# Loads of x behind later weight pieces, and half of its scaling on POOL, in a one-core hybrid retention and attention layer

## The chip, the core and the metric

The kernel runs on one core of a Trainium2 chip. The core has TensorE (PE, with its weight loads shown apart as PEld), VectorE (DVE), ScalarE (ACT), GpSimd (POOL) and SyncE (SP, which here only issues DMAs). Each engine takes its instructions in the order of its own queue and waits on semaphores for the others. The metric is device time in microseconds (us), smaller is better: the median of several runs.

## The reference

One decoder layer on x of 256 rows by 1024, in float32, with two branches that read the same normalised input:

```
h    = rmsnorm(x, ln_w)
proj = h @ w_in                    # 1024 x 9216: rq rk rv rg | mq mk mv mg | gr gm
ret  = groupnorm(retention(rq, rk, rv)) * silu(rg);  ret = ret @ w_ret_o
mo   = causal_attention(mq, mk, mv, ALiBi) * silu(mg);  mo = mo @ w_moba_o
y    = sigmoid(gr) * ret + sigmoid(gm) * mo
out  = rmsnorm(x + y @ w_out, final_norm_w)
```

Retention has 4 heads (queries and keys of 128, values of 256, chunks of 128 rows) with a fixed decay table. The attention has 8 heads of 128, and 256 rows are one block, so only the causal part of the own block is left.

## The kernel before

**Weights in groups and pieces.** All weights are cut into 24 groups of 512 columns, listed in `groups`. Groups 0 and 1 are the retention values, 2 its queries, 3 its keys, 4 the first half of the attention's queries, and so on. A group is loaded in four pieces of two 128-row blocks each (512 KB). Piece 2.1 below is piece 1 of group 2. The raw piece goes into one of 6 buffers, and `split` turns it into a rounded part wh (ACT, L108) and the remainder wl (DVE, L109). A raw buffer is free for the next load when L109 has read it. Products are three or two matmuls per block, so that the two parts together keep float32 accuracy.

**x before its norm is known.** Groups 0 to 2 are multiplied with x times `ln_w` alone (tiles x0, split in `split_x`), since the row factors rs come later. The rows of x (tile xn, two halves of 128 rows) are loaded by SP behind the second piece of group 1, at L133. `x_stats` squares and sums each half on ACT (L185), and a few tiny instructions make rs (L170 to L175). The values of groups 0 and 1 are scaled with rs when they leave PSUM (vh on ACT at L443, vl on DVE at L445). `x_stats_t` spreads rs over the partitions with two small matmuls and a copy to rsb on DVE (L195).

**x after the norm.** `norm_x(k)` makes the normalised block k of eight: z on DVE (L163, x times `ln_w` times rsb), the rounded part on ACT (L164), the remainder on DVE (L165). They are written to the tile xs, which every group from 3 to 17 reads. The queries of group 2, made from x0, are multiplied with rsb on DVE (L414) and split by L258 on ACT and L259 on DVE.

**PSUM and the order.** A group with flag T makes four outputs of 128 columns (f0 to f3), each in its own buffer of the PSUM pool ps_m, which has four. ACT reads one half of it (L393) and DVE adds the other (L395); then the buffer is free. So f0 of group 3 needs the buffer that f0 of group 2 had. The order of each engine's queue comes from a scheduler that takes the program and reorders it within its dependencies.

Of the kernel before, what the change touches and what calls it, by code (L numbers as in the profile page):

```python
# [23 lines left out]
F32 = mybir.dt.float32  # L24
F32R = mybir.dt.float32r
AF = mybir.ActivationFunctionType
ALU = mybir.AluOpType
# [6 lines left out]
NT = S // P  # L34
# [14 lines left out]
def hybrid_kernel(ctx: ExitStack, tc, xT, x, w_in, gn_w, w_ret_o, w_moba_o, w_out, fn_w, decay, out):  # L49
    nc = tc.nc  # L50
# [26 lines left out]
    def load(g, c):  # L77
        src = groups[g][0].rearrange("(k p) c -> p k c", p=P)
        t = wp.tile([P, 2, GW], F32, name="raw", tag="raw", bufs=6)
        raw[g, c] = t  # L80
        if g == 0:
            for j in range(2):
                k = 2 * c + j
                sx = slice(KT + k * S if k else 0, KT + (k + 1) * S)
                nc.sync.dma_start(xt[:, sx], xT[:, sx])
                for cs in cut(g, k):
                    nc.sync.dma_start(t[:, j, cs], src[:, k, cs])  # L87
        else:
            nc.sync.dma_start(t, src[:, 2 * c:2 * c + 2])
# [33 lines left out]
    lnw = xt[:, :KT]  # L123
# [3 lines left out]
    xn = ac.tile([P, NT, D], F32, name="xn", tag="xn")  # L127
    xr = x.rearrange("(t p) d -> p t d", p=P)
    for c in range(4):
        load(1, c)  # L130
        if c == 1:
            for t in range(NT):
                nc.sync.dma_start(xn[:, t], xr[:, t])  # L133
    dec = ac.tile([P, RET_HEADS * 3 * P], F32, name="dec", tag="dec")

    ident = cst.tile([P, P], F32, name="ident")
# [23 lines left out]
    def norm_x(k):  # L160
        xk, h, l = xt[:, KT + k * S:KT + (k + 1) * S], xs[:, k, 0], xs[:, k, 1]
        z = wk.tile([P, S], F32, name="z", tag="z", bufs=4)
        ins = nc.vector.scalar_tensor_tensor(z, xk, lnw[:, k:k + 1], rsb, op0=ALU.mult, op1=ALU.mult)  # L163
        nc.scalar.activation(h, z, AF.Copy)  # L164
        nc.vector.tensor_sub(l, z, h.bitcast(F32))  # L165
        return ins.ins

    def rsqrt(y, a, tmp):
# [9 lines left out]
    rsb = cst.tile([P, S], F32, name="rsb")  # L178
# [68 lines left out]
    def new_v(n, dt=F32):  # L247
        return ac.tile([P, GW], dt, name=n, tag="v", bufs=8)
# [8 lines left out]
    def split_to(out, a, eng=nc.gpsimd):  # L257
        nc.scalar.activation(out[:, 0], a, AF.Copy)  # L258
        eng.tensor_sub(out[:, 1], a, out[:, 0].bitcast(F32))  # L259
# [128 lines left out]
    def evac_t(g, i, ps):  # L388

        f = (i + 4) if g in (7, 8, 13, 15, 17, 19, 21) else i  # L390

        def halves(out, w=1.0):
            nc.scalar.activation(out, ps[:, 1], AF.Copy, scale=w)  # L393
            if w == 1.0:
                nc.vector.tensor_add(out, ps[:, 0], out)  # L395
            else:
                nc.vector.scalar_tensor_tensor(out, ps[:, 0], w, out, op0=ALU.mult, op1=ALU.add)

        def tmp(n):
            return wk.tile([P, S], F32, name=n, tag=n, bufs=4)  # L400

        if g in (4, 7):
            q = qT[g // 7][:, i]
            halves(q, 1.0 / math.sqrt(P))
            split_to(qs[g // 7][:, i], q[:, P:])
        elif g in (5, 8):
            k = kT[g // 8][:, i]
            halves(k)
            split_to(ks[g // 8][:, i], k)
        elif g in (2, 3):  # L410
            a = (qT if g == 2 else kT)["r"][:, i]
            halves(a)
            if g == 2:
                nc.vector.tensor_mul(a, a, rsb)  # L414
            split_to((qs if g == 2 else ks)["r"][:, i], a if g == 2 else a[:, :P], nc.vector)
        elif g in (12, 13):
            z, sg = tmp("z"), wk.tile([P, S], F32, name="sg", tag="sg", bufs=2)
            halves(z)
            nc.scalar.activation(sg, z, AF.Sigmoid)
            nc.vector.tensor_mul(z, z, sg)  # L420
            nc.vector.tensor_mul(oT[:, f], oT[:, f], z)
        elif g in (14, 15, 16, 17):
            z = tmp("z")
            halves(z)
            if i % 2 == 0:
                gt = new_v("gt")
                G[g // 16, f], G[g // 16, f + 1] = gt[:, :S], gt[:, S:]
            nc.scalar.activation(G[g // 16, f], z, AF.Sigmoid)
        elif g in (18, 19):
            halves(A[:, f])  # L430
            nc.gpsimd.tensor_mul(A[:, f], A[:, f], G[0, f])  # L431
        elif g in (20, 21):
            z = tmp("z")
            halves(z)
            nc.vector.tensor_mul(z, z, G[1, f])
            nc.vector.tensor_add(z, z, A[:, f])
            nc.scalar.activation(yT[:, f, 0], z, AF.Copy)
            nc.vector.tensor_sub(yT[:, f, 1], z, yT[:, f, 0].bitcast(F32))
# [31 lines left out]
    def unit(g, i):  # L470
# [25 lines left out]
        if groups[g][1] == "N":  # L496
            evac_n(g, i, proj_n(g, lambda k: xs[:, k], i))
        else:
            if g == 2:
                a = x0s  # L500
            elif g < 18:
                a = lambda k: xs[:, k]
            elif g < 20:
                a = lambda k: rT[k // 2][:, k % 2]
            else:
                a = lambda k: mT[k // 4][:, k % 4]
            for f in (2 * i, 2 * i + 1):
                evac_t(g, f, proj_t(g, a, f))
# [44 lines left out]
    for g in range(2):  # L553
        for i in range(2):
            stream(g, i)
        if g == 0:
            x_stats()
            nc.sync.dma_start(dec, decay)
        pair = [pm.tile([P, GW], F32, name="ps_m", tag="m") for t in range(NT)] if g else ps0
        last = proj_first(g, pair)  # L560
        for t in range(NT):
            evac_n(g, t, pair[t])
        if g:
            with tc.issue_after(last.ins):
                x_stats_t()
            begun = [norm_x(k) for k in range(KT)][3]
    for g in range(2, NG - 2):
        for i in range(2):
            u = 2 * g + i
            stream(g, i)  # L570
            if u == 38:

                xr = new_v("xr", F32R)
# [22 lines left out]
    for t in range(NT):  # L596
        part, a, s, y, v = (sc[:, t, j:j + 1] for j in range(5))
# [80 lines left out]
```

## Time and profile before

| | |
|---|---|
| median of 3 runs | 304.42 us (303.76 to 304.47) |
| profiled execution, its own time | 305.6 us |
| span of the profiled execution, first to last instruction | 302.7 us |
| mean granted TensorE clock | 0.994 |
| PE busy | 294.2 us (97%) |
| DVE busy | 220.7 us (73%) |
| ACT busy | 191.5 us (63%) |
| POOL busy | 28.6 us (9%) |

The profile is one execution. Its time is 2.9 us more than its span and 1.2 us above the median, so a difference that is worked out from it is added to the median. Times in a timeline count from the span's start. A timeline row gives the start, the time from the first start to the last end of the merged instructions, the engine, the line, the output and input names, and how many were merged; in brackets stands how long the engine sat idle before, and what ended the wait. Rows of one engine can overlap a little, because an instruction starts before the one ahead of it has fully ended: what one costs in a queue is the distance from start to start.

### The profile page before, as it was taken

Reading aid. Unit: us, or ns where it says so; the run is one execution under the profiler, and the core shown is the slowest. Engines: PE = TensorE matmul, PEld = TensorE weight load, DVE = VectorE, ACT = ScalarE, POOL = GpSimd, SP = SyncE. Lnnn points to the kernel's source line nnn. Section 1 sums busy time; section 2 is a strip of 40 time slices with the busy share of each in tenths; the row PEclk is TensorE's granted clock in tenths of the full one; section 3 lists DMA queues with packets and bytes.
Section 4 is the critical chain, followed back from the end, with each engine's and each line's share of the span. In section 5 each row is a group of like instructions: output and inputs, shape, how many; then the busy total and the mean of one; then the engine's idle time right before and its main releaser. Section 6 shows DMA issues by size and latency. Waiting matters only on the chain.

```text
span 302.7 us, 4547 instructions
## 1 busy us (share of the span) xinstructions
PE 294.2 (97%) x1628; PEld 253.1 (84%) x1628; DVE 220.7 (73%) x402; ACT 191.5 (63%) x365; POOL 28.6 (9%) x36
## 2 busy tenths in 40 slices
PE   8999989999999999999999999999999999999992
PEld 4768878999888899888888888888888888888891
DVE  3849999977699695884747899557657458899342
ACT  5778695665738676675965857757847626646231
POOL 3000000231200123200000000000000245000000
PEclk9999999999999999999999999999999999999997
DMA  6999847948174461735267185484475576440011
GB/s 184 340 397 410 309 136 222 316 154 240 51 260 126 162 209 71 246 113 197 56 221 237 44 261 146 149 279 120 157 228 174 158 252 229 143 142 1 0 69 69
DMA packets 28966, 55.08 MB, mean 182 GB/s; under 512 B 1936, under 2 KB 3984, under 8 KB 28944
## 3 DMA queue, kind: packets, MB, share of 16 engines
q1 hardware_dynamic: 28624, 54.54, 55.4%
q8 instruction: 12, 0.20, 0.3%
q10 hardware_dynamic: 288, 0.26, 0.2%
q14 instruction: 10, 0.08, 0.1%
q0 software_dynamic: 32, 0.00, 0.0%
HBM read 53.75 MB, written 1.05 MB: 181 GB/s over the span
## 4 chain that ended last, share of the span: by engine, by line
PE 89%; DMA 4%; ACT 3%; SPq 1%; DVE 1%; issue 1%; DVEq 0%; ACTq 0%
PE ps_m L233 37%; PE ps_m L234 19%; PE ps_m L218 7%; PE ps_m L220 7%; PE ps_m L219 7%; DMA raw<-in_w_in 2%; ACT wh L108 2%; DMA xt<-in_xT 2%; PE ps_m L206 1%; PE ps_m L207 1%; PE ps_m L205 1%; PE ps_t L285 1%; SPq L87 1%; ACT xs L164 1%; PE ps_s L264 1%
## 5 line engine op out<-in xcount | busy, mean ns | idle before, releaser
L233 PE MATMUL ps_m<-xs,wh 128*128 128x512 f32 x352 | 123.6, 393 | 0.8 <-ACT qT L393 0.8
L109 DVE TENSOR_TENSOR wl<-raw,wh 128x1024 fp32r<-128x1024 f32 x88 | 108.8, 1256 | 12.9 <-ACT wh L108 12.6
L234 PE MATMUL ps_m<-xs,wl 128*128 128x256 f32 x352 | 98.9, 282 | 0.0
L108 ACT ACTIVATE wh<-raw 128x1024 fp32r<-128x1024 f32 x88 | 90.5, 1053 | 7.2 <-DMA raw<-in_w_in 2.6
L233 PEld LDWEIGHTS ps_m<-xs,wh 128*128 128x128 f32 x352 | 66.0, 188 | 14.5 <-ACT qT L393 1.1
L234 PEld LDWEIGHTS ps_m<-xs,wl 128*128 128x128 f32 x352 | 66.5, 189 | 0.2
L218 PE MATMUL ps_m<-wh,xs 128*128 128x512 f32 x64 | 25.5, 398 | 0.0
L219 PE MATMUL ps_m<-wl,xs 128*128 128x512 f32 x64 | 25.3, 395 | 0.0
L220 PE MATMUL ps_m<-wh,xs 128*128 128x512 f32 x64 | 25.3, 395 | 0.0
L233 PE MATMUL ps_m<-rT,wh 128*128 128x512 f32 x64 | 22.2, 390 | 0.0
L233 PE MATMUL ps_m<-mT,wh 128*128 128x512 f32 x64 | 22.2, 390 | 0.0
L395 DVE TENSOR_TENSOR z<-ps_m,z 128x256 f32<-128x256 f32 x32 | 13.4, 419 | 11.8 <-ACT z L393 11.7
L393 ACT ACTIVATE z<-ps_m 128x256 f32<-128x256 f32 x32 | 12.1, 379 | 13.1 <-PE ps_m L234 12.9
L431 POOL TENSOR_TENSOR A<-A,gt 128x256 f32<-128x256 f32 x8 | 6.8, 855 | 120.1 <-DVE A L395 120.1
L234 PE MATMUL ps_m<-rT,wl 128*128 128x256 f32 x64 | 18.0, 282 | 0.0
L234 PE MATMUL ps_m<-mT,wl 128*128 128x256 f32 x64 | 18.0, 282 | 0.0
L220 PEld LDWEIGHTS ps_m<-wh,xs 128*128 128x128 f32 x64 | 12.0, 188 | 2.9
L206 PE MATMUL ps_m<-wl,x 128*128 128x512 f32 (+1 forms) x34 | 13.7, 404 | 0.5 <-DVE wl L109 0.5
L219 PEld LDWEIGHTS ps_m<-wl,xs 128*128 128x128 f32 x64 | 12.0, 188 | 2.5
L218 PEld LDWEIGHTS ps_m<-wh,xs 128*128 128x128 f32 x64 | 12.0, 188 | 2.5
L233 PEld LDWEIGHTS ps_m<-mT,wh 128*128 128x128 f32 x64 | 12.0, 188 | 2.5
L233 PEld LDWEIGHTS ps_m<-rT,wh 128*128 128x128 f32 x64 | 12.0, 188 | 2.5
(183 smaller groups left out, 487.2 us busy)
## 6 DMA issues: line engine op xcount, KB each, us to landing
raw<-in_w_in SPq DMA_DIRECT2D x68, 512.0 KB, 4.7
raw<-in_w_ret_o SPq DMA_DIRECT2D x8, 512.0 KB, 5.2
raw<-in_w_moba_o SPq DMA_DIRECT2D x8, 512.0 KB, 5.7
raw<-in_w_out SPq DMA_DIRECT2D x8, 512.0 KB, 5.2
raw<-in_w_in SPq DMA_DIRECT2D x7, 256.0 KB, 4.6
xn<-in_x SPq DMA_DIRECT2D x2, 512.0 KB, 8.6
xt<-in_xT SPq DMA_DIRECT2D x7, 128.0 KB, 4.7
dec<-in_decay SPq DMA_DIRECT2D x1, 768.0 KB, 9.3
```

The source lines that it names most:

```text
L87: nc.sync.dma_start(t[:, j, cs], src[:, k, cs])
L108: nc.scalar.activation(h, r, AF.Copy)
L109: nc.vector.tensor_sub(l, r, h.bitcast(F32))
L206: nc.tensor.matmul(ps[:, cs], xh, l, start=False, stop=False)
L218: nc.tensor.matmul(ps, a(k)[:, 0, sl], h, start=not begun and k == 0, stop=False)
L219: nc.tensor.matmul(ps, a(k)[:, 0, sl], l, start=False, stop=False)
L220: nc.tensor.matmul(ps, a(k)[:, 1, sl], h, start=False, stop=k == KT - 1)
L233: nc.tensor.matmul(ps, h, a(k), start=k == 0, stop=False)
L234: nc.tensor.matmul(ps[:, 0], l, a(k)[:, 0], start=False, stop=k == KT - 1)
L393: nc.scalar.activation(out, ps[:, 1], AF.Copy, scale=w)
L395: nc.vector.tensor_add(out, ps[:, 0], out)
L431: nc.gpsimd.tensor_mul(A[:, f], A[:, f], G[0, f])
```

## The change

SP loads the first half of the rows of x behind the third piece of group 1, and the second half behind the fourth. `norm_x` keeps its form for blocks 0 to 3. For blocks 4 to 7, z is x times rsb on POOL, and `ln_w` goes in as a scale of the ACT instruction and as the scalar of a three-operand DVE instruction, which replaces the plain subtraction. The product of group 2's queries with rsb goes from DVE to POOL.

```diff
     for c in range(4):
         load(1, c)
-        if c == 1:
-            for t in range(NT):
-                nc.sync.dma_start(xn[:, t], xr[:, t])
+        if c >= 2:
+            nc.sync.dma_start(xn[:, c - 2], xr[:, c - 2])
...
         z = wk.tile([P, S], F32, name="z", tag="z", bufs=4)
-        ins = nc.vector.scalar_tensor_tensor(z, xk, lnw[:, k:k + 1], rsb, op0=ALU.mult, op1=ALU.mult)
-        nc.scalar.activation(h, z, AF.Copy)
-        nc.vector.tensor_sub(l, z, h.bitcast(F32))
+        if k < 4:
+            ins = nc.vector.scalar_tensor_tensor(z, xk, lnw[:, k:k + 1], rsb, op0=ALU.mult, op1=ALU.mult)
+            nc.scalar.activation(h, z, AF.Copy)
+            nc.vector.tensor_sub(l, z, h.bitcast(F32))
+        else:
+            ins = nc.gpsimd.tensor_mul(z, xk, rsb)
+            nc.scalar.activation(h, z, AF.Copy, scale=lnw[:, k:k + 1])
+            nc.vector.scalar_tensor_tensor(l, z, lnw[:, k:k + 1], h.bitcast(F32), op0=ALU.mult, op1=ALU.subtract)
         return ins.ins
...
             if g == 2:
-                nc.vector.tensor_mul(a, a, rsb)
+                nc.gpsimd.tensor_mul(a, a, rsb)
             split_to((qs if g == 2 else ks)["r"][:, i], a if g == 2 else a[:, :P], nc.vector)
```

The scheduler orders the queues anew. Lines behind the first edit are one lower in the changed kernel, and from the second half of `norm_x` on four higher. ACT's queue from the pieces of group 1 to the first values, before (wh is a weight piece, junk the squares of one half of x, vh the values):

```order
L108 ACTIVATE wh<-raw 128x1024 x2
L185 ACTIVATE junk,ss<-xn 128x1024 x2
L170 ACTIVATE sst<-ss 128x2
L108 ACTIVATE wh<-raw 128x1024
L443 ACTIVATE vh<-ps_m,rs 128x512
```

And now:

```order
L108 ACTIVATE wh<-raw 128x1024 x3
L189 ACTIVATE junk,ss<-xn 128x1024
L108 ACTIVATE wh<-raw 128x1024
L189 ACTIVATE junk,ss<-xn 128x1024
L174 ACTIVATE sst<-ss 128x2
L108 ACTIVATE wh<-raw 128x1024
L447 ACTIVATE vh<-ps_m,rs 128x512
```

Two weight pieces have gone ahead of the second square. DVE's queue from the last pieces of group 2 to the first queries of group 2 that leave PSUM and what follows them, before (vl is the remainder of the values, xs that of the normalised x, wl that of a weight piece, rqs that of the queries):

```order
L445 SCALAR_TENSOR_TENSOR vl<-ps_m,rs,vh 128x512
L109 TENSOR_TENSOR wl<-raw,wh 128x1024
L445 SCALAR_TENSOR_TENSOR vl<-ps_m,rs,vh 128x512
L195 COPY rsb<-ps_s 128x256
L163 SCALAR_TENSOR_TENSOR z<-xt,rsb 128x256 x4
L109 TENSOR_TENSOR wl<-raw,wh 128x1024
L165 TENSOR_TENSOR xs<-z,xs 128x256 x4
L163 SCALAR_TENSOR_TENSOR z<-xt,rsb 128x256 x3
L165 TENSOR_TENSOR xs<-z,xs 128x256 x2
L163 SCALAR_TENSOR_TENSOR z<-xt,rsb 128x256
L109 TENSOR_TENSOR wl<-raw,wh 128x1024
L165 TENSOR_TENSOR xs<-z,xs 128x256 x2
```

And now, with the rows up to the next pieces of group 3:

```order
L449 SCALAR_TENSOR_TENSOR vl<-ps_m,rs,vh 128x512 x2
L199 COPY rsb<-ps_s 128x256
L163 SCALAR_TENSOR_TENSOR z<-xt,rsb 128x256 x3
L165 TENSOR_TENSOR xs<-z,xs 128x256 x3
L163 SCALAR_TENSOR_TENSOR z<-xt,rsb 128x256
L109 TENSOR_TENSOR wl<-raw,wh 128x1024
L165 TENSOR_TENSOR xs<-z,xs 128x256
L169 SCALAR_TENSOR_TENSOR xs<-z,xt,xs 128x256 x3
L109 TENSOR_TENSOR wl<-raw,wh 128x1024
L169 SCALAR_TENSOR_TENSOR xs<-z,xt,xs 128x256
L399 TENSOR_TENSOR qT<-ps_m,qT 128x256 x2
L109 TENSOR_TENSOR wl<-raw,wh 128x1024
```

Both vl stand now behind the last piece of group 2, four z are gone, and the L395 of before, which stood behind its last row, is L399. POOL's queue had nothing between the last row of its preparations (L144) and the remainders of group 4's queries. Now it has eight instructions there:

```order
L143 AFFINE_SELECT rel<-rel 128x256
L167 TENSOR_TENSOR z<-xt,rsb 128x256 x4
L418 TENSOR_TENSOR qT<-qT,rsb 128x256 x4
L263 TENSOR_TENSOR early<-qT,early 128x128 x4
L263 TENSOR_TENSOR mk0s<-kT,mk0s 128x256 x4
```

The four z come before the four products of the queries.

## Rows read from the trace of the kernel before

**Rows 1.** The page's first section: busy us, share of the span, instructions.

```profile
PE 294.2 (97%) x1628; PEld 253.1 (84%) x1628; DVE 220.7 (73%) x402; ACT 191.5 (63%) x365; POOL 28.6 (9%) x36
```

**Rows 2.** Waits of PE: us in total, times, longest.

```profile
PE ps_m L233 <- ACT qT L393: 0.8, 1, 0.8
PE ps_m L206 <- DVE wl L109: 0.5, 1, 0.5
```

**Rows 3.** Timeline of PE at the start of group 3.

```profile
42.17 0.47 PE L233 MATMUL ps_m<-xs,wh 128*128 128x512 f32 x1 [0.79 <-ACT qT L393]
...
42.60 0.40 PE L233 MATMUL ps_m<-xs,wh 128*128 128x512 f32 x1
...
42.95 0.39 PE L233 MATMUL ps_m<-xs,wh 128*128 128x512 f32 x1
43.18 0.28 PE L234 MATMUL ps_m<-xs,wl 128*128 128x256 f32 x1
```

**Rows 4.** Stretch of 39 to 42 us: length, busy of PE, PEld, DVE, ACT, POOL; clock.

```profile
39.00:42.00 3.00, 2.39 (x14) 1.84 (x12) 3.00 (x8) 3.00 (x8) 0.00 (x0) 1.00 0.13 48
```

**Rows 5.** Timeline of DVE, 29.8 to 46 us.

```profile
29.89 0.74 DVE L445 SCALAR_TENSOR_TENSOR vl<-ps_m,rs,vh 128x512 fp32r<-128x512 f32 x1
30.83 1.23 DVE L109 TENSOR_TENSOR wl<-raw,wh 128x1024 fp32r<-128x1024 f32 x1 [0.19 <-ACT wh L108]
31.97 0.75 DVE L445 SCALAR_TENSOR_TENSOR vl<-ps_m,rs,vh 128x512 fp32r<-128x512 f32 x1
32.63 0.42 DVE L195 COPY rsb<-ps_s 128x256 f32<-128x256 f32 x1
33.08 1.67 DVE L163 SCALAR_TENSOR_TENSOR z<-xt,rsb 128x256 f32<-128x256 f32 x4
35.04 1.23 DVE L109 TENSOR_TENSOR wl<-raw,wh 128x1024 fp32r<-128x1024 f32 x1 [0.28 <-ACT wh L108]
36.18 1.43 DVE L165 TENSOR_TENSOR xs<-z,xs 128x256 fp32r<-128x256 f32 x4
...
41.61 0.75 DVE L395 TENSOR_TENSOR qT<-ps_m,qT 128x256 f32<-128x256 f32 x2
42.28 0.75 DVE L414 TENSOR_TENSOR qT<-qT,rsb 128x256 f32<-128x256 f32 x2
42.95 1.22 DVE L109 TENSOR_TENSOR wl<-raw,wh 128x1024 fp32r<-128x1024 f32 x1
...
44.75 1.22 DVE L109 TENSOR_TENSOR wl<-raw,wh 128x1024 fp32r<-128x1024 f32 x1
```

**Rows 6.** Timeline of ACT, 18 to 35.5 us.

```profile
18.98 1.06 ACT L185 ACTIVATE junk<-xn 128x1024 f32<-128x1024 f32 x1 [0.19 <-DMA xn<-in_x]
...
20.32 1.06 ACT L185 ACTIVATE junk<-xn 128x1024 f32<-128x1024 f32 x1 [0.18 <-DMA xn<-in_x]
...
21.81 1.04 ACT L108 ACTIVATE wh<-raw 128x1024 fp32r<-128x1024 f32 x1
23.00 0.69 ACT L443 ACTIVATE vh<-ps_m,rs 128x512 fp32r<-128x512 f32 x1
...
34.91 1.32 ACT L164 ACTIVATE xs<-z 128x256 fp32r<-128x256 f32 x4
```

**Rows 7.** The page's section on DMA issues: KB each, median us to landing.

```profile
xn<-in_x SPq DMA_DIRECT2D x2, 512.0 KB, 8.6
```

**Rows 8.** Timeline of POOL.

```profile
58.80 2.54 POOL L259 TENSOR_TENSOR early<-qT,early 128x128 fp32r<-128x128 f32 x1 [55.70 <-ACT early L258]
...
234.18 0.74 POOL L431 TENSOR_TENSOR A<-A,gt 128x256 f32<-128x256 f32 x1 [109.52 <-DVE A L395]
...
242.48 1.65 POOL L431 TENSOR_TENSOR A<-A,gt 128x256 f32<-128x256 f32 x1 [2.78 <-DVE A L395]
```

**Rows 9.** Timeline of DVE beside POOL's instruction at 242.48.

```profile
242.32 2.90 DVE L109 TENSOR_TENSOR wl<-raw,wh 128x1024 fp32r<-128x1024 f32 x2
```

## The prediction

> **What bounds the kernel now.** The page comes first: PE is busy 294.2 of 302.7 us [rows 1], so work on another engine counts only where PE waits for it. The list of waits, read for PE alone, shows two in the body [rows 2]: 0.5 us inside group 1 and 0.8 us at the first matmul of group 3. The first hangs on piece 1.0, which both kernels load ahead of x, so I leave it. The second is where the change works. In PE's timeline the matmul at 42.17 stood idle for 0.79 [rows 3]: group 2 was done at 41.38. The row names ACT, but the PSUM buffer it writes is f0 of group 2, and this is free only when DVE has added its half. DVE does that in the first of the two L395 at 41.61 [rows 5]. One of them lasts about 0.42 (two take 0.75, 0.33 from start to start), so it ends at 42.03, and PE starts 0.14 later. DVE is busy for all of 39 to 42 [rows 4]: its queue from the copy of rsb (32.63) to that L395 sets the start of group 3. Since PE waits nowhere else up to the end of its work, the change can win 0.79 us there at most, and loses what it makes that queue longer.
>
> **The loads of x.** Both squares on ACT waited for their half of x, at 18.98 and 20.32 [rows 6]: the loads land in the order of issue, one 512 KB piece every 1.3 us. Now the second half lands behind two more weight pieces, so its square moves from 20.32 to about 22.9. SP may stop for a raw buffer ahead of it, but a half of x lands 8.6 us after its issue [rows 7], and such a stop hides in that backlog. From the second square to the first vh took 2.68 us (23.00 less 20.32), so vh comes at 25.6. What hides this: PE is in group 1 until the values of group 1 leave at 29.89 [rows 5], and nothing of rs is needed before. What is late next is DVE. It starts piece 2.0 at 25.6 and has three pieces (1.14 from start to start, 30.83 to 31.97) and two vl (0.66, 31.97 to 32.63) ahead of it: 25.6 + 3.42 + 1.32 = 30.3. Before, one vl of group 1 fitted in at 29.89, ahead of piece 2.3, which waits for ACT until 30.83 in both. Now that vl stands behind it: copy of rsb at 30.83 + 1.14 + 2 x 0.66 = 33.29, **0.66 us later**.
>
> **The scaling of x.** DVE loses four z (0.40 each; four take 1.67) and keeps four remainders in a three-operand form, which I take at the same 0.40 instead of 0.35 (L165, four in 1.43): by itself -1.6 + 0.2 = -1.4 us. POOL gets four products of 128x256. The same form took it 0.74 where DVE left it alone, and 1.65 where DVE ran two L109 [rows 8]. In that place DVE needed 2.90 for two L109 [rows 9], against 1.14 + 1.22 = 2.36 for a pair without POOL: each cost the other time, DVE 0.54. z, xs and L109 all read two operands from SBUF, as that L109 does, so the row fits them. The price of one meeting is thus bounded by 0 (POOL falls into a wait of DVE's) and 0.74 (DVE stands still for all of it). I take 0.54, the nearest row.
>
> The Trainium skill, page "SBUF — State Buffer", section "Who interferes with whom", says that a DVE instruction with two SBUF inputs and a GpSimd instruction that reads SBUF exclude each other, and that the second waits for all of the first. The trace agrees that they meet and that POOL waits, but DVE lost 0.54 and not 0.74. By the page each of five full meetings counted here would cost 0.2 more, an estimate of 1.0 us on top of the sum.
>
> The walk down DVE's new queue: copy at 33.29, first z 0.45 later (32.63 to 33.08) at 33.74. Three z with two of POOL's four cutting in: 1.20 + 1.08, to 36.02. ACT has the rounded parts by then (from 34.91 on [rows 6]). Three remainders with POOL's other two: 1.05 + 1.08, to 38.15. Then z (0.40), piece 3.0 (1.14), one remainder (0.35), three of the new form (1.20), piece 3.1 (1.14), the last new one (0.40): 42.78. The first L399 ends 0.42 later at 43.20 and PE starts at 43.34 instead of 42.17: **+1.2 us**. Where POOL loses the race instead, DVE ends up waiting at a remainder for POOL's z and ACT's rounding, and the same 2 us appear as a wait. Queued behind that remainder are piece 3.1, the L399 and with it PE, and SP's loads, which need the raw buffers that L109 frees; those loads are for group 4, more than 10 us away.
>
> **The products of the queries.** DVE loses four L414, 0.67 per pair from start to start: two stood between L395 (41.61) and piece 3.2 (42.95). The L263 behind piece 3.2 now waits for POOL and then ACT. Walk: the second L399 is followed at 42.78 + 0.66 = 43.44 by piece 3.2, but POOL has begun the first product when the first L399 landed, at 43.3, so I count 0.4 of a meeting: 43.84 to 44.98. The second product then cuts in, runs 0.74 to 45.72, and ACT rounds it by 46.15. The two L263 start at 45.5 and 46.2, and piece 3.3 starts at 46.55, ending 1.22 later at 47.77; before it ended at 45.97. By the new order PE has nine pairs of L237 and L238 and one L237 of group 3 ahead of the first matmul that needs that remainder. A pair is 0.35 (42.60 to 42.95 [rows 3]), one L237 0.23: 43.34 + 3.38 = 46.72. It waits 1.05 us, where before there was none: **+1.05**. From there PE has 23 more pairs of group 3 to do, 8 us, in which DVE has only its two pairs of queries and the first pieces of group 4 to deliver; I count no third wait.
>
> **Sum.** 1.17 + 1.05 = +2.2 us on the profiled 305.6: 307.8. On the median: 304.42 + 2.2 = **306.6 us**. Unknown ends: with all meetings free the walk gives -0.4 (below), with one long starvation +4.0.
>
> **Rivals.**
> - *The offload is free.* POOL's products fall between DVE's instructions. For it: four of them alone take 3.0 us, DVE has 8 us to the remainders. Against it: the only such meeting with L109 that I read cost 0.54. Walk without meetings: the three z end at 34.94, DVE waits for ACT's first part at 34.91 + 0.40 = 35.3, the rest is 6.1 us (1.05 + 0.40 + 1.14 + 0.35 + 1.20 + 1.14 + 0.40 + 0.42) to 41.4, PE starts at 41.55: -0.6. Piece 3.3 then ends at about 45.1, PE wants it at 44.93: +0.2. Total -0.4: 304.0, not slower. It decides once the meetings cost under 0.2 each. The whole 0.79 back, 303.6, is its end.
> - *POOL starves.* At 58.80 half the size took 2.54 us, while DVE ran one instruction behind the other [rows 8]. Once in the chain of the last z or the second product this adds up to 2.54 - 0.74 = 1.8 us: 308.4. Against it: at 242.48 POOL was let in after one L109.
> - *Only the first wait grows.* The second needs PE to reach piece 3.3 early. If DVE makes up 1 us there, +1.2 stays: 305.6.
>
> **Chances.** Forecast 0.45; starvation 0.15; first wait only 0.15; free offload 0.20; all 0.79 back or more, 0.05. About 0.3%, 0.9 us, is what a measurement can tell from no change. Slower by more: most of the forecast and of starvation, two thirds of the third case: 0.70. Within: the free offload and the rest: 0.23. Faster by more needs over 0.9 us, more than the wait at 42.17 holds: 0.07. The range runs from the free offload to starvation, 304.0 to 308.4. The likeliest case alone is 305.6 to 307.6.
>
> **What would show it.** In the changed profile: the second square at about 22.9 and the copy of rsb at about 33.3; POOL's z lasting over 0.74 each, and DVE's z and xs rows longer than 0.40 each when merged; the first matmul of group 3 at 43 to 44 with an idle time near 2 us; a second wait of PE, near 1 us, for a wl of group 3, some 3.4 us later. From there on both timelines should run parallel. The forecast is wrong if POOL's z take 0.74 and PE starts group 3 before 42.2, or if a wait of PE appears in group 1 or 2. The clock stayed at 1.00 over the wait of 0.79 [rows 4]; whether it stays over 2 us no row shows, and a lower one after it would push the time above the forecast.

## The result, and the profile after

The changed kernel takes **307.69 us** (306.93 to 308.07, four runs) against 304.42 (303.76 to 304.47): a ratio of 1.0109, 95% interval 1.0086 to 1.0133. It is slower by 3.27 us, where +2.2 was forecast; 307.69 lies inside the range of 304.0 to 308.4, and just above the 305.6 to 307.6 that the prediction gave to its likeliest case alone. The profiled execution took 306.93 at a mean clock of 0.998, with a span of 305.1.

The page's busy line answers to [rows 1]. PE does the same 1628 matmuls in the same busy time; POOL has gained 7 us.

```profile
PE 294.0 (96%) x1628; PEld 253.9 (83%) x1628; DVE 222.4 (73%) x394; ACT 192.3 (63%) x365; POOL 35.7 (12%) x44
```

The list of waits for PE, with us in total, times and longest, answers to [rows 2]. The wait of 0.8 at the start of group 3 is now 2.9, and a second one, for a remainder of a weight piece of group 3, is new.

```profile
PE ps_m L237 <- DVE qT L399: 2.9, 1, 2.9
...
PE ps_m L238 <- DVE wl L109: 0.6, 1, 0.6
```

Before two timelines are laid beside each other their zero has to be made equal. The first loads land at a different time in each run, whatever the kernel. PE starts group 2 at 30.02 in the trace of before and at 28.79 in that of after, 1.23 earlier, and up to there it runs the same matmuls. So 1.23 is added to a time of after wherever it is compared. PE's timeline of before, the rows not shown so far:

```profile
30.02 0.48 PE L233 MATMUL ps_m<-x,wh 128*128 128x512 f32 x1
...
100.16 0.49 PE L285 MATMUL ps_t<-ident,tS 128*128 128x128 f32 x3
```

PE's timeline of after, which answers to [rows 3]:

```profile
28.79 0.48 PE L237 MATMUL ps_m<-x,wh 128*128 128x512 f32 x1
...
43.05 0.47 PE L237 MATMUL ps_m<-xs,wh 128*128 128x512 f32 x1 [2.88 <-DVE qT L399]
...
44.51 0.39 PE L237 MATMUL ps_m<-xs,wh 128*128 128x512 f32 x1
44.85 0.39 PE L238 MATMUL ps_m<-xs,wl 128*128 128x256 f32 x1
45.08 0.39 PE L237 MATMUL ps_m<-xs,wh 128*128 128x512 f32 x1
...
47.49 0.39 PE L238 MATMUL ps_m<-xs,wl 128*128 128x256 f32 x1 [0.63 <-DVE wl L109]
...
102.12 0.49 PE L289 MATMUL ps_t<-ident,tS 128*128 128x128 f32 x3
```

Two stretches hold nearly all of the loss. Group 3 starts 2.11 later (43.05 + 1.23 - 42.17), and 2.09 of that is the wait, 2.88 against 0.79. From there to the first transpose PE needs 59.07 (102.12 less 43.05) where it needed 57.99 (100.16 less 42.17): 1.08 more. Most of this is the second wait: the matmul at 47.49 starts 0.91 after the one ahead of it (46.58), where 0.12 is usual (the row's 0.63 counts from that one's end). The matmuls at 44.51 and 44.85 also took 0.34 and 0.23 from start to start, against 0.23 and 0.12 elsewhere. Together the two stretches are 3.19. Behind the first transpose PE's timeline is as long as before: its last matmul comes 196.32 after it in both traces. Only the end of the program behind that matmul is longer, 6.7 us (305.1 less 298.44) where it was 6.2 (302.7 less 296.48). It is 6.6 to 6.7 in all four profiles that hold the whole change with z in its shared buffers, and 6.2 in the ten others. The compute rows of that end are as before; why its closing semaphores come later is not known.

DVE's timeline answers to [rows 5].

```profile
32.06 0.41 DVE L199 COPY rsb<-ps_s 128x256 f32<-128x256 f32 x1
32.51 1.28 DVE L163 SCALAR_TENSOR_TENSOR z<-xt,rsb 128x256 f32<-128x256 f32 x3
34.81 1.65 DVE L165 TENSOR_TENSOR xs<-z,xs 128x256 fp32r<-128x256 f32 x3 [1.03 <-ACT xs L164]
36.38 0.96 DVE L163 SCALAR_TENSOR_TENSOR z<-xt,rsb 128x256 f32<-128x256 f32 x1
37.26 1.77 DVE L109 TENSOR_TENSOR wl<-raw,wh 128x1024 fp32r<-128x1024 f32 x1
...
39.29 1.74 DVE L169 SCALAR_TENSOR_TENSOR xs<-z,xt,xs 128x256 fp32r<-128x256 f32 x3
...
42.49 0.74 DVE L399 TENSOR_TENSOR qT<-ps_m,qT 128x256 f32<-128x256 f32 x2
...
46.21 1.22 DVE L109 TENSOR_TENSOR wl<-raw,wh 128x1024 fp32r<-128x1024 f32 x1
```

Two things are to be seen. Instructions that met POOL are too long: three remainders 1.65 instead of 1.10, one z 0.96 instead of 0.48, a piece 1.77 instead of 1.22, three of the new form 1.74 instead of 1.27 (what they take without POOL is shown below, in the kernel with POOL's work on DVE). That is four meetings at 0.51 on average, 2.05 us. And ahead of the first remainder DVE stood idle for 1.03, where it had 0.28 before piece 3.0 in [rows 5].

The timeline of POOL in that stretch, which was empty before:

```profile
35.32 2.62 POOL L167 TENSOR_TENSOR z<-xt,rsb 128x256 f32<-128x256 f32 x3 [32.22 <-DVE xs L165]
39.44 0.91 POOL L167 TENSOR_TENSOR z<-xt,rsb 128x256 f32<-128x256 f32 x1 [1.50 <-DVE xs L165]
42.98 2.41 POOL L418 TENSOR_TENSOR qT<-qT,rsb 128x256 f32<-128x256 f32 x2 [2.62 <-DVE qT L399]
```

POOL's first z does not start when rsb is there (32.47) but at 35.32, released by DVE's first remainder. All z share four buffers, and the first z of POOL is the fifth: it takes the buffer of the first, which this remainder frees.

ACT's timeline answers to [rows 6]:

```profile
21.72 1.06 ACT L189 ACTIVATE junk<-xn 128x1024 f32<-128x1024 f32 x1 [0.19 <-DMA xn<-in_x]
...
33.14 0.39 ACT L397 ACTIVATE qT<-ps_m 128x256 f32<-128x256 f32 x1 [3.01 <-PE ps_m L238]
33.42 1.05 ACT L108 ACTIVATE wh<-raw 128x1024 fp32r<-128x1024 f32 x1
34.37 1.02 ACT L164 ACTIVATE xs<-z 128x256 fp32r<-128x256 f32 x3
```

The second square comes at 21.72 + 1.23 = 22.95, where 22.9 was forecast. The first rounding of z, on which DVE waits, stands in ACT's queue behind the first queries of group 2 that leave PSUM and behind a weight piece. So it starts at 34.37 whenever z is there. In the time of before that is 35.60, 0.69 later than the 34.91 of [rows 6]: by PE's new order f0 of group 2 ends 4.35 after the group's start (28.79 to 33.14) and not 3.65 (30.02 to 33.67), as the matching row of before in ACT's timeline has it:

```profile
33.67 0.39 ACT L393 ACTIVATE qT<-ps_m 128x256 f32<-128x256 f32 x1 [2.30 <-PE ps_m L234]
```

### The profile page after: what moved, and what is told of

Its sections match the earlier page's. It is cut to its first block, busy times and chain, and to the rows that moved or that the text cites. A ratio compares the mean times of both kernels' runs of the same rounds, so it can differ in the third digit from the quotient of the medians.

```text
span 305.1 us, 4548 instructions
## 1 busy us (share of the span) xinstructions
PE 294.0 (96%) x1628; PEld 253.9 (83%) x1628; DVE 222.4 (73%) x394; ACT 192.3 (63%) x365; POOL 35.7 (12%) x44
## 3 DMA queue, kind: packets, MB, share of 16 engines
HBM read 53.75 MB, written 1.05 MB: 180 GB/s over the span
## 4 chain that ended last, share of the span: by engine, by line
PE 93%; DVE 4%; POOL 1%; ACT 1%; issue 0%; DVEq 0%; ACTq 0%
PE ps_m L237 36%; PE ps_m L238 19%; PE ps_m L222 7%; PE ps_m L224 7%; PE ps_m L223 7%; PE ps_m L210 3%; PE ps_m L209 3%; PE ps_m L211 3%; DVE wl L109 1%; PE ps_s L117 1%; PE ps_t L289 1%; POOL qT L418 1%; DVE xs L169 1%; DVE xs L165 1%; PE ps_s L268 1%; PE ps_o L308 1%
## 5 line engine op out<-in xcount | busy, mean ns | idle before, releaser
L109 DVE TENSOR_TENSOR wl<-raw,wh 128x1024 fp32r<-128x1024 f32 x88 | 110.4, 1272 | 13.2 <-ACT wh L108 12.9
L399 DVE TENSOR_TENSOR z<-ps_m,z 128x256 f32<-128x256 f32 x32 | 13.4, 420 | 11.8 <-ACT z L397 11.7
L222 PE MATMUL ps_m<-wh,yT 128*128 128x512 f32 (+1 forms) x40 | 14.0, 350 | 0.0
```

The lines of the kernel that those rows point to most:

```text
L109: nc.vector.tensor_sub(l, r, h.bitcast(F32))
L222: nc.tensor.matmul(ps, a(k)[:, 0, sl], h, start=not begun and k == 0, stop=False)
```

## The experiments

Each kernel's median stands against runs of the kernel before that were timed beside it. "First wait" is PE's wait at group 3 (0.79 before, 2.88 after), "stretch" the time from that matmul to the first transpose (57.99 before, 59.07 after); neither depends on when the first loads land.

### Which part costs what

**Only the loads of x.** The kernel before with this edit alone:

```diff
-        if c == 1:
-            for t in range(NT):
-                nc.sync.dma_start(xn[:, t], xr[:, t])
+        if c >= 2:
+            nc.sync.dma_start(xn[:, c - 2], xr[:, c - 2])
```

> Only the loads of x move; all scaling stays on DVE as before. My walk: the copy of rsb comes 0.66 us later, nothing else in DVE's queue grows, so the first matmul of group 3 waits 0.7 us longer: 305.1 us. Rival 1, the loads are hidden: 304.4 us, the wait at group 3 stays 0.8. Rival 2, the loads are what costs the change its 3.3 us: over 307 us.

Measured 307.11 against 304.08, ratio 1.0096 (1.0066 to 1.0125): +3.03 and not the 305.1 expected. The number is that of the second rival, though only half of it turns out to be a wait. The first wait is 2.15, which is +1.36; rsb is copied 0.66 later, as in the whole change. The rest is in DVE's timeline: the same idle time of 1.02 ahead of the first remainder.

```profile
35.68 1.10 DVE L164 TENSOR_TENSOR xs<-z,xs 128x256 fp32r<-128x256 f32 x3 [1.02 <-ACT xs L163]
```

0.66 and 0.74 (1.02 less 0.28) make 1.40. Moving two loads has also moved weight piece 3.0 behind the remainders in the scheduler's order, and it is missing from the gap that it filled. That the new order makes the idle time is read from these rows; no run holds the loads moved and the order as it was. The stretch takes 59.53, +1.54, with no second wait. There the page's windows (length, busy of PE, PEld, DVE, ACT and POOL, granted clock, DMA) show another cause:

```profile
42.00:43.00 1.00, 0.00 (x0) 0.00 (x0) 1.00 (x3) 1.00 (x2) 0.00 (x0) 1.00 0.83 152
...
44.00:45.00 1.00, 1.00 (x5) 0.85 (x4) 1.00 (x2) 0.58 (x3) 0.00 (x0) 0.50 0.64 119
...
47.00:48.00 1.00, 1.00 (x6) 0.91 (x6) 1.00 (x4) 0.55 (x1) 0.00 (x0) 0.83 0.62 225
```

After the wait the granted clock fell to 0.50, which is 1.2 of 2.4 GHz, until about 47.3. The 1.54 is thus no wait but slower matmuls, and it is tested below.

**Only the scaling on POOL.** The kernel before with `norm_x` of the changed kernel.

> Only half of the scaling of x moves to POOL; loads and queries as before. Theory: POOL's first z waits for DVE's first remainder, because all z share four buffers, and then three or four of POOL's products meet DVE instructions at 0.54 us each. First matmul of group 3 about 0.9 us later than in the kernel before: 305.3 us, no second wait. Rival, POOL's work is free beside DVE: 303.9 us.

Measured 305.18 against 304.08, ratio 1.0048 (1.0033 to 1.0063). That is close to the 305.3 expected. First wait 1.54 (+0.75), stretch 58.21. DVE's timeline shows piece 3.0 back in its gap, and the meetings behind it: four remainders take 2.52 instead of 1.43, a piece 1.76 instead of 1.22, four of the new form 2.15.

```profile
34.42 1.23 DVE L109 TENSOR_TENSOR wl<-raw,wh 128x1024 fp32r<-128x1024 f32 x1 [0.30 <-ACT wh L108]
35.56 2.52 DVE L166 TENSOR_TENSOR xs<-z,xs 128x256 fp32r<-128x256 f32 x4
38.00 1.76 DVE L109 TENSOR_TENSOR wl<-raw,wh 128x1024 fp32r<-128x1024 f32 x1
39.68 2.15 DVE L170 SCALAR_TENSOR_TENSOR xs<-z,xt,xs 128x256 fp32r<-128x256 f32 x4
```

**Only the queries on POOL.**

```diff
-                nc.vector.tensor_mul(a, a, rsb)
+                nc.gpsimd.tensor_mul(a, a, rsb)
```

> Only the product of group 2's queries with rsb moves to POOL. Theory: the wait at the first matmul of group 3 stays 0.8 us, and DVE waits for POOL and ACT at the remainders of the queries, so that the last wl piece of group 3 comes some 0.7 us later and PE waits up to 0.5 us more: 304.9 us. Rival, hidden: 304.4 us. Rival, this alone makes the second wait of 1 us: 305.4 us.

Measured 305.21 against 304.08, ratio 1.0035 (1.0019 to 1.005), between the 304.9 of the theory and the 305.4 of the last rival. The trace decides for that rival: the first wait is unchanged, the second is there by itself, and the stretch takes 59.08 (+1.09):

```profile
41.74 0.47 PE L233 MATMUL ps_m<-xs,wh 128*128 128x512 f32 x1 [0.79 <-ACT qT L393]
...
46.18 0.39 PE L234 MATMUL ps_m<-xs,wl 128*128 128x256 f32 x1 [0.62 <-DVE wl L109]
```

**The whole change with POOL's work on DVE.** Loads and the three-operand form stay; both products go back to DVE.

```diff
-            ins = nc.gpsimd.tensor_mul(z, xk, rsb)
+            ins = nc.vector.tensor_mul(z, xk, rsb)
...
-                nc.gpsimd.tensor_mul(a, a, rsb)
+                nc.vector.tensor_mul(a, a, rsb)
```

> The changed kernel with everything that went to POOL back on DVE, in the new form (product with rsb first, the weights as a scale on ACT and in the three-operand remainder), and the loads moved. Theory: no meetings, but DVE has 2.8 us of work back and its wait for ACT; near the kernel with the moved loads alone: 306 to 307.3 us. If POOL's work were the main cause of the loss, this would be far below the changed kernel: 305 us.

Measured 306.45 against 303.99, ratio 1.0074 (1.0051 to 1.0097). First wait 2.16, as with the loads alone; stretch 57.98.

```profile
33.18 0.41 DVE L199 COPY rsb<-ps_s 128x256 f32<-128x256 f32 x1
...
35.93 1.09 DVE L165 TENSOR_TENSOR xs<-z,xs 128x256 fp32r<-128x256 f32 x3 [1.02 <-ACT xs L164]
36.94 0.48 DVE L163 SCALAR_TENSOR_TENSOR z<-xt,rsb 128x256 f32<-128x256 f32 x1
37.34 1.09 DVE L167 TENSOR_TENSOR z<-xt,rsb 128x256 f32<-128x256 f32 x3
...
38.68 1.27 DVE L169 SCALAR_TENSOR_TENSOR xs<-z,xt,xs 128x256 fp32r<-128x256 f32 x3
...
42.88 0.75 DVE L399 TENSOR_TENSOR qT<-ps_m,qT 128x256 f32<-128x256 f32 x2
```

The profile's clock stayed up, and its waits make +1.37. The median stands 1.1 higher. Two of the four runs had a mean clock of 0.991 and 0.992, which is part of it; but the other two, at 0.998 and 0.997, lie 1.96 and 2.30 above the kernel before, so some 0.6 to 0.9 stay open. The offload doesn't relieve DVE: from the copy of rsb to the first L399 it has 9.70 us here and 10.43 with the offload, and the first wait is 0.72 longer with it. POOL takes four products of 0.34 off DVE's queue, 1.4 us as forecast, and 2.1 come back in meetings. The waits in the profiles add up: 1.36 + 0.75 + 1.09 = 3.20, and the whole change shows 2.09 + 1.08 = 3.17. The medians of the parts do not (3.03 + 1.10 + 1.13 = 5.26), since half of what the loads alone cost is the clock.

### The price of a meeting, and the buffers of z

**Four products on POOL that nobody reads.** The kernel before with POOL reading x and rsb just when DVE begins its z; all of the computation stays.

```diff
+            spare = new_qk("spare")
+            for k in range(4):
+                nc.gpsimd.tensor_mul(spare[:, k], xt[:, KT + k * S:KT + (k + 1) * S], rsb)
             begun = [norm_x(k) for k in range(KT)][3]
```

> The kernel before, with four more products of x and rsb on POOL behind the copy of rsb, whose results nobody reads: POOL work of the same size as in the change, on which nobody waits. DVE's queue is that of before. Theory: each product meets DVE's instructions with two SBUF inputs and costs DVE 0.54 us; the first matmul of group 3 comes 1.5 to 2.2 us later and its wait of 0.8 grows to 2.3 to 3.0: 305.6 to 306.3 us, about 1 us more where the granted clock falls behind the long wait. Rival, POOL costs only through those who wait for it: 304.1 us.

Measured 306.68 against 304.40, ratio 1.0079 (1.0056 to 1.0102). Nothing waits for these four, so what they cost is the meeting alone. DVE's timeline, with 1.67 and 1.23 in [rows 5]:

```profile
31.94 3.13 DVE L163 SCALAR_TENSOR_TENSOR z<-xt,rsb 128x256 f32<-128x256 f32 x4
34.99 1.76 DVE L109 TENSOR_TENSOR wl<-raw,wh 128x1024 fp32r<-128x1024 f32 x1
```

1.46 and 0.53: 2.0 for four, 0.50 each, next to the 0.54 that [rows 8, 9] gave. PE's first wait is 2.38 (+1.59, since DVE's idle time of 0.28 ahead of piece 3.0 is used up), the stretch behind it 59.38 (+1.39), where the clock fell once more. Together that is 2.98, more than the 2.28 between the medians; the difference is not placed.

```profile
42.00:45.00 3.00, 2.36 (x7) 2.11 (x8) 3.00 (x8) 2.95 (x6) 0.00 (x0) 0.54 0.60 175
```

The Trainium skill, page "SBUF — State Buffer", section "Who interferes with whom", has a DVE instruction with two SBUF inputs contend with a GpSimd instruction that reads SBUF, and calls the contention an exclusive lock. Taken as DVE standing still for all of POOL's 0.74, that is an estimate of 3.0 us for the four; the trace shows 2.0, so it agrees that the two meet and not on the price.

**Own buffers for POOL's z.** The whole change, with POOL's four z in a tile of their own.

```diff
+    zp = None
...
-        z = wk.tile([P, S], F32, name="z", tag="z", bufs=4)
+        nonlocal zp
+        if k == 4:
+            zp = new_qk("zp")
+        z = zp[:, k - 4] if k >= 4 else wk.tile([P, S], F32, name="z", tag="z", bufs=4)
```

> The whole change, with the four z of POOL in a tile of their own. Theory: in the changed kernel POOL's first z started only at 35.3, after DVE's first remainder, though rsb was there at 32.5, because all z share four buffers; DVE meanwhile sat idle for 1.03 us. With own buffers POOL starts near 32.6, and the chain to group 3 is about 1 us shorter: 306.7 us. Rival, only the meetings on the port cost: the same number of meetings, 307.7 us.

Measured 305.68 against 304.08, ratio 1.0054 (1.0036 to 1.0073): 2.0 under the changed kernel's 307.69, or 1.7 if each is counted from the runs beside it, and more than the 1.0 that the theory gave. First wait 1.67 (1.21 less), stretch 58.66 (0.41 less), and the end of the program is back at 6.2 (0.4 less). POOL starts behind the copy of rsb, and its products cut into DVE's z from the first on, as the walk had it:

```profile
32.76 3.68 POOL L172 TENSOR_TENSOR zp<-xt,rsb 128x256 f32<-128x256 f32 x4 [29.65 <-DVE rsb L204]
```

DVE has no idle time there. But the scheduler, freed of the buffer, also put ACT's first rounding ahead of the queries; it starts as soon as z is there:

```profile
33.23 0.42 ACT L169 ACTIVATE xs<-z 128x256 fp32r<-128x256 f32 x1 [1.29 <-DVE z L168]
```

Which of the two is worth how much of the 2.0, this run doesn't tell.

### What PE waits for

**Other PSUM buffers for group 3.** The kernel before, with f0 and f1 of group 3 in the second PSUM pool, so that they need no buffer that DVE has to free.

```diff
-        ps = pm.tile([P, 2, S], F32, name="ps_m", tag="m")
+        if g == 3 and i < 2:
+            ps = pa.tile([P, 512], F32, name="ps_s", tag="s").rearrange("p (a s) -> p a s", a=2)
+        else:
+            ps = pm.tile([P, 2, S], F32, name="ps_m", tag="m")
```

> The kernel before, with the first two outputs of group 3 in the PSUM buffers of the scores, which are free then. If the wait of 0.8 us at group 3 is for the buffer that DVE has still to read (the step the prediction names), it goes and nothing takes its place: 303.3 us against 304.1. Rival, the normalised x or ACT holds group 3 up, as the row's releaser says: 304.1 us, the wait stays.

Measured 303.88 against 304.40, ratio 0.9985 (0.9968 to 1.0002). PE goes from group 2 to group 3 without a wait:

```profile
41.06 0.28 PE L237 MATMUL ps_m<-x,wl 128*128 128x256 f32 x1
41.18 0.39 PE L236 MATMUL ps_s<-xs,wh 128*128 128x512 f32 x1
```

That settles that the 0.79 was the buffer. The time was not settled, so the same kernel was timed again.

> The kernel before with the first two outputs of group 3 in buffers of the other PSUM pool, unaltered from its first run and timed a second time against the kernel before, since there the wait of 0.79 us was gone from the trace and the time 0.15% lower with an interval that touched no change. If the whole wait comes back as time: 0.6 to 0.8 us under before, a ratio of 0.9975 to 0.998. If something behind it takes it back, which one profile need not show: 1.000.

Measured 303.61 against 304.07, ratio 0.9983 (0.9967 to 0.9998). Two timings give 0.52 and 0.46 us, the second with an interval that just excludes no change: most likely this kernel beats both others by about half a microsecond. It isn't the full 0.79. The stretch takes 58.31 and 58.80 in the two profiles instead of 57.99; a wait of 0.27 for ACT shows in the second, the rest is not placed.

**The same buffers in the changed kernel.**

> The changed kernel with the same two outputs of group 3 in the buffers of the scores. Theory: DVE's queue is what is late in the changed kernel, and the wl pieces of group 3 in it take over as the thing waited for: the wait of 2.9 us breaks up into three, and about 0.9 us is won: 306.0 to 306.8 us, with no fall of the clock. Rival, the PSUM buffer alone is what costs: 304.9 us or less.

Measured 307.81 against 304.40, ratio 1.0097 (1.0068 to 1.0126): nothing won, though a gain of about 0.9 was expected. PE enters group 3 at once, and then stops at the weight pieces instead:

```profile
43.48 0.39 PE L241 MATMUL ps_s<-xs,wl 128*128 128x256 f32 x1 [1.14 <-DVE wl L109]
...
48.75 0.38 PE L241 MATMUL ps_s<-xs,wl 128*128 128x256 f32 x1 [0.74 <-DVE wl L109]
```

A third wait, of 0.55, comes at L346. From the start of group 2 to the first transpose it is 73.34, against 73.33 in the changed kernel (102.12 less 28.79). There DVE's queue as a whole is late, and the buffer was only where it was seen first.

### The clock

**The changed kernel once more**, unaltered.

> The changed kernel once more, unaltered, to part two reasons for its spread. Theory: every run carries 2.1 us more of wait at group 3 and 1.1 more inside it, counted from the first rounding of group 1, and the start shifts all of it by up to 1.3 us: 307.6 us, whether the clock falls or not in the profiled run; if it falls, the profile shows some 1.4 us more behind the wait. Rival, without a fall of the clock it is 306.9 us and only with one 307.7: runs with a mean clock of 0.995 and more then lie below 307.

Measured 308.48 (306.75 to 310.17, six runs) against 303.99, ratio 1.0127 (1.0095 to 1.0158). The first wait is again 2.87, but in this profile the clock fell behind it:

```profile
42.00:45.00 3.00, 0.29 (x1) 0.30 (x2) 3.00 (x7) 2.94 (x5) 0.38 (x2) 1.00 0.52 165
45.00:48.00 3.00, 3.00 (x13) 2.57 (x12) 2.80 (x4) 1.34 (x3) 2.05 (x2) 0.61 0.77 191
```

The stretch takes 59.53, without a second wait: the slower PE comes to piece 3.3 when it is ready. So in the changed kernel the fall costs only 0.46 on top of the 59.07 and not the 1.4 expected, because it uses up the 1.08 that would have been a wait. The median missed both values expected; it is 0.79 above that of the first four runs, and six runs of one kernel spread over 3.4 us, which nothing here explains.

**Matmuls in the wait.** With the loads alone, six matmuls of the warm-up (1.47 us, into a buffer nobody reads) are put between groups 2 and 3; all of the computation stays.

```diff
+FILL = 6
...
+            tail[:] = [nc.tensor.matmul(ps[:, 0], l, a(k)[:, 0], start=False, stop=k == KT - 1).ins]
...
+            if u == 6:
+                with tc.issue_after(tail[0]):
+                    pf = pa.tile([P, 512], F32, name="ps_s", tag="s")
+                    for j in range(FILL):
+                        nc.tensor.matmul(pf, warm[:, :P], warm, start=True, stop=True)
```

> The kernel with the moved loads alone (all scaling on DVE), with six matmuls on the warm-up tile, about 1.4 us, in its wait of 2.15 us before group 3. In that kernel the granted clock fell to half behind the wait and cost 1.5 us between the first matmul of group 3 and the first transpose at about 100 us. Theory, PE's idleness brings the fall about: with the filler the clock stays at 1.00 and the time is 305.6 us. Rival, it has another cause: 307.0 us and a clock of 0.5 in the same stretch.

Measured 305.55 against 303.99, ratio 1.0042 (1.0026 to 1.0059): +1.56, where the loads alone were +3.03. Group 3 starts no sooner (10.25 after the copy of rsb in both); the stretch is back at 58.00, and the clock at 1.00 all through:

```profile
40.22 1.47 PE L589 MATMUL ps_s<-warm 128*128 128x512 bf16 x6
42.53 0.48 PE L234 MATMUL ps_m<-xs,wh 128*128 128x512 f32 x1 [0.84 <-DVE qT L396]
```

```profile
42.00:45.00 3.00, 2.47 (x14) 2.19 (x15) 3.00 (x8) 2.33 (x4) 0.00 (x0) 1.00 0.77 231
45.00:48.00 3.00, 3.00 (x19) 2.65 (x19) 3.00 (x7) 1.36 (x3) 0.00 (x0) 1.00 0.77 254
```

One profile could have kept its clock by chance, but the mean clocks of the runs say the same. With the loads alone it was 0.991 in three of four runs, and the one at 0.996 took 305.81; with the filler it was 0.993 or more in all eight. A mean clock of 0.992 or less shows only in the kernels with a first wait of 2.15 or more and no filler, and there in 15 of 22 runs; no run of the others whose clock is on record has it, the kernel before included.

**The same with eight matmuls (1.90 us) in the changed kernel.**

> The changed kernel with eight matmuls on the warm-up tile between group 2 and group 3, into a free buffer, 1.7 us of PE work inside the wait of 2.9 us. Theory: in the kernel with the moved loads alone, the granted clock fell to half for some 3.4 us behind a PE wait of 2.15 us, and the mean clock of three of the four runs of the changed kernel says that it fell there too; with PE kept at work the clock stays, and the time is that of the run without a fall, 306.9 us, in all runs. Rival, the spread of the runs is from the loads at the start: 307.7 us as before.

Measured 307.64 against 304.40, ratio 1.0113 (1.0093 to 1.0132): no gain, as the rival had it. The clock stayed at 1.00, but the second wait is there (0.98) and ends 4.45 behind the start of group 3, as in the profile of the changed kernel (4.44). Keeping the clock up only lets PE come earlier to a piece that is late. Behind it the stretch lost another 0.35 that is not placed.

## Why the prediction was right, and where its size failed

- **Direction and place: right.** Both losses sit where the text put them: at the first matmul of group 3 and at a remainder of group 3, 4.44 later (43.05 to 47.49; 3.38 + 1.05 was forecast). The idle time at the first was 2.88, where near 2 was forecast.
- **The loads of x: right up to the copy of rsb.** It comes at 32.06 + 1.23 = 33.29, the forecast 33.29, the second square at 22.95 against 22.9. But 0.66 is not all that the loads cost: alone they lengthen the first wait by 1.36, the other half through the new order behind that copy.
- **Price of a meeting: right.** 0.46 to 0.55 for each product of x and rsb in four kernels, in the stretches of z, xs and L109 alike, where 0.54 was taken. POOL did not starve: in the changed kernel its z took 0.85 to 0.92 each, and the second product of a pair of queries 1.72, a wait for one DVE instruction that the walk had counted.
- **The products of the queries: right.** +1.05 forecast; 1.08 measured, and 1.09 with this part alone. (What the text calls 0.4 of a meeting adds 0.40 us to piece 3.2 in its walk; with this part alone that piece took 1.65 instead of 1.22.)
- **The step that failed: the walk down DVE's queue from the copy of rsb to the first L399, in "The scaling of x".** It said +0.51 there beyond the 0.66, and 1.45 was measured (42.49 less 32.06 is 10.43, against 8.98). It let POOL's first two products cut into DVE's three z and counted ACT's rounding as ready from 34.91 on. POOL could not start, since it shares the buffers of z, and the rounding came at 35.60. So DVE first stood idle for 1.03 and then had all four meetings. The text held the two for alternatives ("the same 2 us appear as a wait"), and they came one behind the other. Besides, it took the idle time as POOL's doing; the loads alone show it too. The meetings came at 2.05 where the walk had 2.16; the term that was missing is the idle time. 1.17 + 0.94 = 2.11, by which group 3 starts later.
- **The clock.** The prediction said that no row showed it over a wait of 2 us and that a fall would push the time above the forecast. It falls in some executions. In the changed kernel it adds 0.46, as one profile against another shows. In that kernel's first four runs the mean clock was 0.998, 0.991, 0.990 and 0.994, so two of them may hold a fall. The 3.19 of the two waits, the 0.4 at the end and this make somewhat more than the 3.27 between the medians; they were not separated from the scatter of the start.
- **The rivals.** A free offload (304.0) and the whole 0.79 back fall with the meetings of 0.50; starvation and "only the first wait" fall with the rows above.
- **What was luck.** The 0.94 that the walk missed moves the forecast to the edge of its likeliest case (305.6 to 307.6), and 307.69 lies just past it. That it is still inside the range is owed to an upper end that was put there for a starvation which did not come.

## What to carry to other kernels

Before you price an instruction moved to another engine, list what it shares with those it leaves: here a pool of four buffers and operands in SBUF made POOL start late and cost DVE more than the work it took away. When a load moves, read the whole new order of the engine that sets the end, and look for the instruction that used to fill a gap: a piece of 1.14 us gone from a gap costs what the gap then holds. And when PE's waits grow, price the clock behind them as well as the wait.

## What was not expected of the hardware

The granted clock fell from 1.00 to 0.50 behind a single wait of PE of 2.15, 2.38 and 2.87 us, though no wait of PE ahead of it was longer than 1.2 us and the granted clock had been 1.00; in the trace of the loads alone it stayed there until about 47.3. It cost 1.54 and 1.39 us where no second wait lay behind. It did not fall behind 0.79, 1.54 and 1.67 us, and, in other profiles, not behind 2.16 and 2.88: the same wait does it in one execution and not in the next. The Trainium skill, page "TensorE: Matmul & The Clock Gate", section "Part 1: The HAM clock gate", tells of a gate that halves the clock by how busy PE has lately been; the traces agree on the two levels, and with six matmuls of no use in the wait the higher one stayed. What parts the executions in which the clock fell from those in which it did not, no run here shows.
